# Query products in two column parts, and expert-table products 352 to 400 columns wide, in a two-layer PEER trunk

## The chip, the cores and the metric

The kernel runs on one core of one Trainium2 chip, as one program. The metric is the device time of one execution in microseconds (us), from launch to the last write; smaller is better. One execution was also taken by the hardware profiler, and all rows of a profile below come from that one.

## The reference

The kernel computes two decoder layers for 512 tokens of width 1024. Each layer is a mixer (gated linear attention with memory attention in the first layer, stick-breaking attention with memory attention in the second), a residual with layer norm, and then a PEER feed-forward: every token picks 128 of 16384 experts by product keys and adds up their outputs. The part that matters here, cut down:

```python
def peer(x, w_q, subkeys, u_tab, v_tab):            # x: 512 x 1024
    q = (xf @ w_q).reshape(N, 8, 2, 128)            # 2048 query columns: 16 blocks of 128
    s = einsum('nhpd,hpkd->nhpk', q, subkeys)       # scores against 16 x 128 sub-keys
    top_s, top_i = top_k(s, 16)                     # product keys: 16 x 16 candidates, best 16
    ...
    g = softmax(best_s)
    act = gelu(einsum('nd,nhkd->nhk', xt, u_tab[it]))     # u_tab, v_tab: 16384 x 1024
    return einsum('nhk,nhkd->nd', g * act, v_tab[it])
```

## The kernel before

**How PEER is done.** The kernel treats the tokens in two ways. The first 128 tokens, and 32 of the next 128, gather their experts' rows by indirect DMA and use VectorE. For the other 352 tokens (`TU = 352`, tokens `TU0 = 160` to 511) the product with u's table is done in full on TensorE: all 16384 rows of u, as 128 blocks of 128 rows (`P = 128` blocks), against the 352 tokens. Which experts count, and with what weight, comes in later through gate matrices that are built from one-hot products (`pg`). The v table is then multiplied with the weighted activations for 384 tokens.

**How a product is split.** Each float32 operand is held as a high and a low part of type fp32r (`xhi`, `xlo` for the tokens; `uh`, `ul` for a block of a weight table, made by `split` on ScalarE and VectorE). `stat_mm` computes one block as 24 products: eight 128-row chunks `c` of the contraction, and for each chunk high times high (line 117), high times low (118) and low times high (119). In each of these the block of the weight table is the stationary operand (a weight load of 128 x 128 goes ahead of every product), and the tokens are the moving operand. "Columns" of a product are the columns of the moving operand, that is tokens: 512 for the query products `pq`, 352 for u's products `ph`. `sl` cuts a range out of the columns of both the tokens and the PSUM bank.

**Order of the work.** Per layer there are a stage of query products (16 blocks `pq`, each followed one turn later by four score products `pss` with the sub-keys; the first three blocks, `LEAD = 3`, are done in two halves of 256 columns as the layer norm ahead of them finishes), a stage of u blocks (`ublock(b)`, with the VectorE selection work, the gate products `pg` and the row gathers paced in between by `Stream` budgets), and a stage of v blocks (products `acc`, 512 columns). In the u stage the order on VectorE, ScalarE and TensorE is the order in which the code is written. All 24 products of a block write one PSUM bank of 512 float32 columns (`ps`, 8 banks), which ScalarE reads when the block is done: `query(pn)` for a query block, and a GELU over `ph[:, :TU]` one turn later for a u block.

**Names in the rows.** `pq<-xhi,uh` is a query product, `ph<-xhi,uh` one of u's, `acc` one of v's, `pz` a logit product of the stick-breaking attention (64 rows deep, two at a time on the two halves of the rows), `bsp` and the like are input projections.

Of the kernel before, what the change touches and what calls it, by code (L numbers as in the profile page):

```python
# [18 lines left out]
T = 512  # L19
# [12 lines left out]
def new_x(E):  # L32

    E.xhi = E.xp.tile([P, NC, T], F32R, tag="xhi", name="xhi")
    E.xlo = E.xp.tile([P, NC, T], F32R, tag="xlo", name="xlo")


def setup(ctx, tc):
# [19 lines left out]
    new_x(E)  # L58
    E.raw = ctx.enter_context(tc.tile_pool(name="raw", bufs=RB))
    E.hl = ctx.enter_context(tc.tile_pool(name="hl", bufs=3))  # L60
# [14 lines left out]
def psum(E, name="ps", tag="ps"):  # L75
    p, tags = E.ps
    return p.tile([P, 512], F32, tag=tag, name=name, bufs=tags[tag])
# [31 lines left out]
def stat_mm(E, ps, hi, lo, xhi=None, xlo=None, sl=slice(None), cs=range(NC)):  # L109

    nc = E.nc
    xhi = E.xhi if xhi is None else xhi
    xlo = E.xlo if xlo is None else xlo
    ps = ps[:, sl]
    for c in cs:
        h, l = hi[:, c * P:(c + 1) * P], lo[:, c * P:(c + 1) * P]
        nc.tensor.matmul(ps, h, xhi[:, c, sl], start=(c == 0), stop=False)  # L117
        nc.tensor.matmul(ps, h, xlo[:, c, sl], start=False, stop=False)  # L118
        nc.tensor.matmul(ps, l, xhi[:, c, sl], start=False, stop=(c == NC - 1))  # L119
# [121 lines left out]
def out_proj_ln(E, cat, wo, lng, lnb, ahead, order, w, rows=None):  # L241
# [3 lines left out]
    with E.tc.tile_pool(name="lp", bufs=1, reuse_waits="tile") as lp:  # L245
# [6 lines left out]
        with E.tc.manual_schedule(engines={mybir.EngineType.PE}):  # L252
            accs = [[psum(E, name="oacc") for h in range(2)] for t in range(2)]

            def add(t, cs):
                for c in cs:
                    ch, cl = cat[c]
                    mov_mm(E, accs[t], ch[:, t * P:(t + 1) * P], cl[:, t * P:(t + 1) * P], *w[c], c == order[0], c == order[-1])
# [8 lines left out]
            for t in range(2):  # L267
                add(t, order[2:WOI])
            for t in range(NT + 1):
                if t < 2:  # L270
                    add(t, order[WOI:])
                elif t < NT:
                    accs.append([psum(E, name="oacc") for h in range(2)])
                    add(t, order[:WOI])
                    x_to_T(E, t - 2)
                    add(t, order[WOI:])
                else:
# [717 lines left out]
def x_to_T(E, t, tag="ps"):  # L995

    nc = E.nc
    for g in range(2):
        ps = psum(E, name="xtp", tag=tag)
        for j in range(4):  # L1000
            c = g * 4 + j
            nc.tensor.transpose(ps[:, j * P:(j + 1) * P], E.x[:, t, c * P:(c + 1) * P], E.ident)
        hi = E.xhi[:, g * 4:(g + 1) * 4, t * P:(t + 1) * P]
        lo = E.xlo[:, g * 4:(g + 1) * 4, t * P:(t + 1) * P]
        psv = ps.rearrange("p (j n) -> p j n", j=4)
        nc.scalar.activation(hi, psv, AF.Copy)
        nc.vector.tensor_sub(lo, psv, hi.bitcast(F32))
# [56 lines left out]
TU0 = T0 + SD  # L1064
TU = T - TU0
# [22 lines left out]
LEAD = 3  # L1088
TAIL = 6
G3 = 96  # L1090
WARM = 6
WOI = 3
RB = 4
SEG = [(0, 1, 0, 16), (1, 3, 16, 8), (4, 4, 40, 4), (8, 8, 56, 1)]

# [15 lines left out]
def peer(E, mixer, wq, sk, ut, vt, un, lng, lnb, out_dram=None, follow=()):  # L1111
# [11 lines left out]
    with ExitStack() as pp:  # L1123
        parts = {}

        def prep(i, later=None):

            if i >= 16 + P:
                return
            parts[i] = split(E, load_raw(E, wq[i] if i < 16 else ut[i - 16], "ur"), "u", later=later)  # L1130
# [124 lines left out]
        with ExitStack() as up:  # L1255
# [383 lines left out]
            def select(row):  # L1639

                on = [sel for sel in sels if row < ER or sel is not sels[2]]
                topk16(*[sel.job() for sel in on[:2]])
                if on[2:]:
                    topk16(on[2].job())
                if row % 8 == 7:
                    for sel in on:
                        lead.q.append(candidates(sel))
                        if sel is first and sel.nr == 8:
                            lead.q.append(first.part(0, 4))
                return WF - 1140 - 1175 * len(on)  # L1650

            def query(pq):
                qT = wk.tile([P, T], F32, tag="act", name="qT")
                nc.scalar.activation(qT, pq, AF.Copy)
                return qT

            def scores(r, qT):
                pss = psum(E, name="pss")
                for t in range(NT):
                    nc.tensor.matmul(pss[:, t * P:(t + 1) * P], qT[:, t * P:(t + 1) * P], skt[:, r], start=True, stop=True)  # L1660
                return lambda: nc.scalar.activation(sall[:, r].rearrange("p t k -> p (t k)"), pss, AF.Copy)

            def flush():
                while later:
                    later.pop(0)(V)
# [4 lines left out]
            for r in range(17):  # L1670
                if r < 16:
                    if r < LEAD:
                        pn = pes[r]
                    else:
                        hi, lo = parts.pop(r)
                        pn = psum(E, name="pq")
                        stat_mm(E, pn, hi, lo)
                if r > 0:
                    ev = scores(r - 1, qT)
                if r + 2 >= LEAD:  # L1680
                    prep(r + 2, later if r > 1 else None)
                if r < 16:
                    qT = query(pn)
                if r > 0:
                    ev()
                if r > 1:
                    avail[0] = r - 1
                    lead(select(r - 2))
                    flush()
                    gus(GQ)  # L1690
# [7 lines left out]
            def ublock(b):  # L1698
                nonlocal ab, ph, big, keep, g0
                if b == KB:  # L1700
                    big = gp.tile([P, 16 * NT * P], F32, tag="big", name="keep")
                    keep = big[:, :KEEP * TU].rearrange("p (b n) -> p b n", n=TU)
                    g0 = big[:, KEEP * TU:KEEP * TU + G0 * TD].rearrange("p (s i n) -> p s i n", i=G0, n=TS)
                if 0 < b <= KB:
                    if (b - 1) % AB == 0:
                        ab = wk.tile([P, AB, TU], F32, tag="act", name="act")
                pn = None
                if b < P:
                    if b > 0:
                        prep(b + 18, later)  # L1710
                    hi, lo = parts.pop(16 + b)
                    pn = psum(E, name="ph")
                    stat_mm(E, pn[:, :TU], hi, lo, E.xhi[:, :, TU0:], E.xlo[:, :, TU0:])
                if b > KB:
                    nc.scalar.activation(keep[:, b - 1 - KB], ph[:, :TU], AF.Gelu)
                elif b > 0:
                    nc.scalar.activation(ab[:, (b - 1) % AB], ph[:, :TU], AF.Gelu)
                    if (b - 1) % AB == AB - 1:
                        nc.scalar.dma_start(Ad[(b - 1) // AB], ab)
                ph = pn  # L1720
                gst(GR if work.q else GR2)
                if lead.q:
                    lead(WB0)
                else:
                    work(WB if ready or sready and len(gst.q) > 1 else WB0)
                flush()
                if b < P - 1:
                    gus(GU if work.q else GU2 if b < KB else GU3)
                if LOG:
                    print("block", b, len(work.q), len(gst.q), len(gus.q), gcount)  # L1730

            for b in range(BX):
                ublock(b)
# [72 lines left out]
        with written:  # L1806
            for b in range(BX, P + 1):
                ublock(b)
                if b < P:
                    vprep(b - BX)  # L1810
# [4 lines left out]
            for b in range(P):  # L1815
# [6 lines left out]
                whi, wlo, hi, lo = vp.pop(b)  # L1822
                for t in range(ND):
                    sl = slice(t * P, (t + 1) * P)
# [21 lines left out]
            for t in range(ND):  # L1846
                sl = slice(t * P, (t + 1) * P)
# [43 lines left out]
def trunk(ctx, tc, a, out):  # L1891
    nc = tc.nc
    E = setup(ctx, tc)
    mix = mixer_a(E, a)
    peer(E, mix, a["wq0"], a["sk0"], a["ut0"], a["vt0"], a["un0"], a["lng1"], a["lnb1"], follow=[a["b_st"][b] for b in (0, 1, 12)])
    mix = mixer_b(E, a["b_st"], a["b_nat"], a["b_wo"], a["lng2"], a["lnb2"])
    peer(E, mix, a["wq1"], a["sk1"], a["ut1"], a["vt1"], a["un1"], a["lng3"], a["lnb3"], out_dram=out)
# [58 lines left out]
```

## Time and profile before

| what | value |
|---|---|
| median of 2 runs | 2854.38 us (2854.05 to 2854.7) |
| the profiled execution's own time | 2856.13 us |
| its span, first to last instruction | 2854.1 us |
| granted TensorE clock, mean over the span | 0.997 |
| TensorE products (PE), busy | 2821.5 us, 99% of the span, 16235 instructions |
| TensorE weight loads (PEld), busy | 2501.9 us, 88% |
| VectorE (DVE) / ScalarE (ACT), busy | 2442.0 us, 86% / 1440.4 us, 50% |
| query stage, first layer | from 227.3 us to 331.0 us |
| u stage, first and second layer | 567.0 us and 570.9 us long |

Products overlap in the profile: one of 512 columns in v's stage is shown as 389 ns long, and the next one starts before it ends. So the step from one product's start to the next one's says what a product costs in a stream, and its duration does not. The source rows give the count, the shortest, median and longest duration, and the start of the first and of the last.

### The profile page before, as it was taken

To read this page: it belongs to the slowest core of one execution; us is meant where nothing else is said; L and a number is where in the kernel's file an instruction comes from. 1 tells how busy PE (TensorE), PEld (TensorE's weight loads), DVE (VectorE), ACT (ScalarE), POOL (GpSimd) and SP (SyncE) were. 2 spreads that over 40 slices of the span, in tenths; PEclk is the share of its full clock that TensorE was granted. 3 is DMA by queue.
4 is the path that set the end of the run, shared out by engine and by line. 5 is a ranking of instruction groups with operands and counts; after the bars stand their busy time and mean duration, and the time that the engine had idled before them with its cause. 6 is when DMAs were issued, how large, how long until landed. Compare 5 with 4: busy or idle time off the path is not lost.

```text
span 2854.1 us, 44772 instructions
## 1 busy us (share of the span) xinstructions
PE 2821.5 (99%) x16235; PEld 2501.9 (88%) x16235; DVE 2442.0 (86%) x4866; ACT 1440.4 (50%) x2699; POOL 754.3 (26%) x615
## 2 busy tenths in 40 slices
PE   9999999999999999999999999999999999999998
PEld 8888999999999888888787889999999998888886
DVE  5566999999987888888968779999998878888888
ACT  6342446667674334443346434476776834334332
POOL 0100233333343333333100002333333433234320
PEclk9999999999999999999999999999999999999999
DMA  5332599999999999999621326999999999999994
GB/s 195 111 104 77 190 314 329 337 333 348 352 375 363 346 371 369 388 359 376 223 67 45 111 82 228 330 314 327 332 350 359 368 369 345 373 348 399 364 377 164
DMA packets 317934, 821.26 MB, mean 288 GB/s; under 512 B 34608, under 2 KB 126992, under 8 KB 311312
## 3 DMA queue, kind: packets, MB, share of 16 engines
q1 hardware_dynamic: 198112, 414.24, 41.0%
q0 software_dynamic: 82944, 302.03, 29.4%
q10 hardware_dynamic: 36656, 102.14, 9.3%
q8 instruction: 127, 2.08, 0.3%
q14 instruction: 95, 0.78, 0.1%
HBM read 723.31 MB, written 92.90 MB: 286 GB/s over the span
## 4 chain that ended last, share of the span: by engine, by line
PE 80%; DVE 16%; issue 2%; ACT 1%; DMA 1%; ACTq 0%; POOL 0%; DVEq 0%; SPq 0%; POOLq 0%
PE acc L289 12%; PE acc L291 12%; PE acc L293 12%; PE ph L117 7%; PE ph L119 7%; PE ph L118 7%; DVE gr L1106 4%; DVE ul L1106 4%; DVE ob L1106 2%; PE pq L117 2%; PE pq L118 2%; PE pq L119 2%; PE pss L1660 1%; PE bsp L117 1%; PE oacc L289 1%
## 5 line engine op out<-in xcount | busy, mean ns | idle before, releaser
L119 PE MATMUL ph<-xhi,ul 128*128 128x352 f32 x2048 | 670.5, 327 | 11.3 <-DVE ul L1106 10.9
L117 PE MATMUL ph<-xhi,uh 128*128 128x352 f32 x2048 | 681.5, 333 | 0.0
L118 PE MATMUL ph<-xlo,uh 128*128 128x352 f32 x2048 | 668.3, 326 | 0.0
L1166 POOL DMA_INDIRECT gr<-in_un,gidx x256 | 344.2, 1345 | 1063.5 <-DVE gr L1106 483.6
L97 ACT ACTIVATE vh<-vr 128x1024 fp32r<-128x1024 f32 x248 | 263.1, 1061 | 521.4 <-PE acc L293 481.4
L1166 POOL DMA_INDIRECT gr<-in_vt,gidx x256 | 297.9, 1164 | 613.7 <-DVE va L1245 550.5
L289 PE MATMUL acc<-vh,whi 128*128 128x512 f32 x1480 | 456.0, 389 | 1.4 <-ACT whi L1801 1.4
L293 PE MATMUL acc<-vh,wlo 128*128 128x512 f32 x1480 | 455.8, 389 | 0.0
L291 PE MATMUL acc<-vl,whi 128*128 128x512 f32 x1480 | 455.8, 389 | 0.0
L98 DVE TENSOR_TENSOR vl<-vr,vh 128x1024 fp32r<-128x1024 f32 x248 | 303.5, 1224 | 144.9 <-ACT vh L97 142.3
L97 ACT ACTIVATE uh<-ur 128x1024 fp32r<-128x1024 f32 x288 | 303.9, 1055 | 243.5 <-PE ph L118 198.9
L119 PEld LDWEIGHTS ph<-xhi,ul 128*128 128x128 f32 x2048 | 385.9, 188 | 17.8 <-DVE ul L1106 17.4
L118 PEld LDWEIGHTS ph<-xlo,uh 128*128 128x128 f32 x2048 | 386.6, 189 | 0.0
L117 PEld LDWEIGHTS ph<-xhi,uh 128*128 128x128 f32 x2048 | 386.3, 189 | 0.1
L1106 DVE TENSOR_TENSOR ul<-ur,uh 128x1024 fp32r<-128x1024 f32 x280 | 340.2, 1215 | 10.2 <-ACT uh L97 9.8
L289 PEld LDWEIGHTS acc<-vh,whi 128*128 128x128 f32 x1480 | 277.5, 188 | 60.3 <-ACT whi L1801 3.1
L293 PEld LDWEIGHTS acc<-vh,wlo 128*128 128x128 f32 x1480 | 277.6, 188 | 58.1 <-DVE wlo L1802 0.7
L291 PEld LDWEIGHTS acc<-vl,whi 128*128 128x128 f32 x1480 | 277.6, 188 | 58.0 <-DVE vl L98 0.8
L1106 DVE SCALAR_TENSOR_TENSOR gr<-gr,xnat 128x1024 f32<-128x1024 f32 x256 | 309.4, 1217 | 20.4 <-DMA gr<-in_un,gidx 20.2
L1245 DVE SCALAR_TENSOR_TENSOR va<-gr,gw,va 128x1024 f32<-128x1024 f32 x254 | 324.7, 1278 | 1.1
L1571 ACT ACTIVATE obl<-ob,rat 128x128 f16<-128x128 f16 x704 | 223.9, 392 | 50.5 <-DVE ob L1106 31.6
L1801 ACT ACTIVATE whi<-w 128x384 fp32r<-128x384 f32 x256 | 131.0, 512 | 68.7 <-DVE w L1790 63.2
(388 smaller groups left out, 4325.2 us busy)
## 6 DMA issues: line engine op xcount, KB each, us to landing
ur<-in_ut SPq DMA_DIRECT2D x256, 512.0 KB
vr<-in_vt SPq DMA_DIRECT2D x256, 512.0 KB
Gd<-gt ACTq DMA_DIRECT2D x48, 1024.0 KB
gl<-Gd SPq DMA_DIRECT2D x26, 1536.0 KB
Ad<-act ACTq DMA_DIRECT2D x112, 352.0 KB
al<-Ad SPq DMA_DIRECT2D x112, 352.0 KB
ur<-in_wq SPq DMA_DIRECT2D x32, 512.0 KB
bs<-in_b_st SPq DMA_DIRECT2D x14, 512.0 KB
```

The costliest lines, as they stand in the source:

```text
L97: nc.scalar.activation(hi, raw, AF.Copy)
L98: sub = lambda eng=eng: eng.tensor_sub(lo, raw, hi.bitcast(F32))
L117: nc.tensor.matmul(ps, h, xhi[:, c, sl], start=(c == 0), stop=False)
L118: nc.tensor.matmul(ps, h, xlo[:, c, sl], start=False, stop=False)
L119: nc.tensor.matmul(ps, l, xhi[:, c, sl], start=False, stop=(c == NC - 1))
L289: nc.tensor.matmul(acc[hf], lh, hi[:, hf * 512:(hf + 1) * 512], start=first, stop=False)
L291: nc.tensor.matmul(acc[hf], lh, lo[:, hf * 512:(hf + 1) * 512], start=False, stop=False)
L293: nc.tensor.matmul(acc[hf], ll, hi[:, hf * 512:(hf + 1) * 512], start=False, stop=last)
L1106: self.ins = op(*args, **kw)
L1166: nc.gpsimd.indirect_dma_start(out=gr, out_offset=None, in_=tab, in_offset=bass.IndirectOffsetOnAxis(ap=idx[:, k:k + 1], axis=0))
L1245: nc.vector.scalar_tensor_tensor(va, gr, gw[:, k:k + 1], va, op0=ALU.mult, op1=ALU.add)
L1571: nc.scalar.activation(obl[:, q], ob[:, q, 0], AF.Copy, scale=rat[:, n0 + q:n0 + q + 1])
```

## The change

Two tables of widths are added, and two calls of `stat_mm` change. Of each layer's 16 query blocks the 13 that were done in one go (`r` from 3 to 15) are now done in two column parts: 24 products over the first `QW[r - LEAD]` columns and then 24 over the rest, with every weight chunk loaded twice. The parts are 320 and 192 columns for the first of them, 336 and 176 for the next, and so on; the wide part has 350.8 columns in the mean and the narrow one 161.2. Each u block takes `n = UW[b % 8]` columns, 352, 356, 360, 364, 368, 376, 384 or 400, the last `n` tokens of the 512; the mean is 370. The PSUM view is then cut to its last 352 columns, so the GELU reads the same tokens as before, and the surplus columns are computed and not read.

```diff
+QW = (320, 336, 304, 288, 272, 352, 344, 328, 368, 384, 400, 416, 448)
+UW = (352, 356, 360, 364, 368, 376, 384, 400)
...
                         pn = psum(E, name="pq")
-                        stat_mm(E, pn, hi, lo)
+                        for sl in (slice(0, QW[r - LEAD]), slice(QW[r - LEAD], T)):
+                            stat_mm(E, pn, hi, lo, sl=sl)
...
+                    n = UW[b % len(UW)]
                     pn = psum(E, name="ph")
-                    stat_mm(E, pn[:, :TU], hi, lo, E.xhi[:, :, TU0:], E.xlo[:, :, TU0:])
+                    stat_mm(E, pn[:, :n], hi, lo, E.xhi[:, :, T - n:], E.xlo[:, :, T - n:])
+                    pn = pn[:, n - TU:]
```

On TensorE, the first whole query block (`r = 3`) stands between two groups of score products. Before it reads as follows (24 products, of which the first three are shown):

```order
L1660 MATMUL pss<-skt,qT 128x128 x8
L117 MATMUL pq<-xhi,uh 128x512
L118 MATMUL pq<-xlo,uh 128x512
L119 MATMUL pq<-xhi,ul 128x512
...
L1660 MATMUL pss<-skt,qT 128x128 x4
```

In the changed kernel the same place holds 24 products of 320 columns and 24 of 192:

```order
L1662 MATMUL pss<-skt,qT 128x128 x8
L117 MATMUL pq<-xhi,uh 128x320
L118 MATMUL pq<-xlo,uh 128x320
L119 MATMUL pq<-xhi,ul 128x320
...
L117 MATMUL pq<-xhi,uh 128x192
L118 MATMUL pq<-xlo,uh 128x192
L119 MATMUL pq<-xhi,ul 128x192
...
L1662 MATMUL pss<-skt,qT 128x128 x4
```

Nothing else moved there. TensorE's program has 624 products more in all (2 layers x 13 blocks x 24). The u blocks hold the same number of products as before, 768 of each of the eight widths over both layers. The order of the instructions on VectorE, ScalarE, GpSimd and SyncE is the same as before.

## The prediction

> **What bounds the kernel now.** I read the page's busy line first, then the stages one by one, since the change touches two of them only.
>
> ```profile
> PE 2821.5 (99%) x16235; PEld 2501.9 (88%) x16235; DVE 2442.0 (86%) x4866; ACT 1440.4 (50%) x2699; POOL 754.3 (26%) x615
> 227.30:331.00 103.70, 103.70 (x594) 91.12 (x593) 84.85 (x410) 36.80 (x54) 7.32 (x7) 1.00 0.34 114
> 331.00:898.00 567.00, 560.40 (x3885) 545.91 (x3884) 532.24 (x1217) 366.31 (x743) 208.97 (x152) 1.00 0.95 341
> 1643.80:1747.50 103.70, 103.70 (x594) 91.12 (x593) 84.85 (x410) 36.80 (x54) 6.38 (x7) 1.00 0.38 120
> 1747.50:2318.40 570.90, 563.03 (x3886) 547.55 (x3885) 530.96 (x1214) 364.51 (x742) 205.60 (x152) 0.99 0.94 339
> PE ph L119 <- DVE ul L1106: 10.9, 14, 1.5
> ```
>
> The four windows are the two query stages and the two u stages. Their columns are length, then busy time with the count of PE, PEld, DVE, ACT and POOL. In the query stages PE is busy for all of 103.70 us, so it waits for nobody there. In the u stages it is idle for 567.00 - 560.40 = 6.6 us and 570.90 - 563.03 = 7.9 us, 14.5 us together, of which the last row puts 10.9 us down to VectorE's low parts `ul`. VectorE is nearly full too (532 of 567 us), but it is TensorE that is late nearly all the time. Whatever the change adds to TensorE's stream in these four windows therefore lengthens the run, less what it takes out of those 14.5 us. So the question is what a product costs as a function of its columns, and the answer has to come from steps between starts.
>
> ```profile
> L118 PE MATMUL pq<-xlo,uh x21: 283/283/283, 237.8 to 245.0; 128*128 128x256 f32 x21
> L118 PE MATMUL pq<-xlo,uh x6: 389/389/389, 255.3 to 258.7; 128*128 128x512 f32 x6
> L118 PE MATMUL ph<-xlo,uh x41: 327/328/328, 339.8 to 359.8; 128*128 128x352 f32 x41
> 550.78 0.32 PE L117 MATMUL ph<-xhi,uh 128*128 128x352 f32 x1
> 554.58 0.32 PE L117 MATMUL ph<-xhi,uh 128*128 128x352 f32 x1
> ```
>
> Every third product of a stream is on line 118, so 21 of them are 60 steps: 256 columns cost 7.2 us / 60 = 120.0 ns. The second row gives 3.4 / 15 = 226.7 ns for 512 columns. From these two, a column costs 106.7 / 256 = 0.4167 ns, and each product has 13.3 ns on top. At 352 columns that line would give 160.0 ns, but the trace has **two rhythms** there. The third row, an undisturbed stretch of 120 steps, gives 20.0 / 120 = 166.7 ns. The last two rows stand 24 products apart in a later stretch and give 3.80 / 24 = 158.3 ns. I call these the slow rhythm (20.0 ns above the columns) and the fast one (11.7 ns above). A stream keeps its rhythm until a wait disturbs it.
>
> The mean over a u stage lies between. The first layer's stage of 567.0 us holds 3072 products of u, and these besides:
>
> ```profile
> 331.00:898.00 567.00, 527.39 (x3071) 502.97 (x3072) 56.72 (x127) 1.00 0.95 341
> L1590 PE MATMUL pg<-ob 128*128 128x128 f16 x704 | 95.8, 221 | 0.0
> 702.78 0.23 PE L1590 MATMUL pg<-ob 128*128 128x128 f16 x1
> 703.21 0.41 PE L117 MATMUL ph<-xhi,uh 128*128 128x352 f32 x1
> 703.46 0.33 PE L118 MATMUL ph<-xlo,uh 128*128 128x352 f32 x1
> ```
>
> The first row is for the tile `ph` alone, with its 3072 weight loads. A gate group is 8 products in 703.21 - 702.78 = 0.43 us, and the step after it is 0.25 us, some 0.08 longer than usual. With 704 such products on this line over both layers, as many on the next, and a few of the side tokens, a layer has about 96 groups (an estimate): 41 + 8 = 49 us. With 9 us for waits (the 6.6 of idle time, and some that the overlap covers) and 1 for transposes, 567 - 59 = 508 us remain, that is 165 ns for each product. So about four fifths of the stream is in the slow rhythm.
>
> **The change, part by part.** *Query blocks.* 13 blocks in each of 2 layers, 24 products each, are 624 products of 512 columns, which become 624 wide and 624 narrow ones. The wide parts have 350.8 columns in the mean: 146.2 ns for the columns, and 160 ns with the 13.3 of the two straight rows. With 11.7 they are 158, with 20 they are 166. The narrow parts (64 to 240 columns, 161.2 in the mean) lie below every width that a full-depth stream of this type has in the trace. What bounds them can be seen in the stick-breaking logits, which are products of 512, 384 and 128 columns with the same kind of weight load:
>
> ```profile
> 1502.20 0.34 PE L788 MATMUL pz<-kqh 64*128 64x384 f32 x2
> 1502.38 0.34 PE L788 MATMUL pz<-kql,kqh 64*128 64x384 f32 x2
> 1502.55 0.34 PE L788 MATMUL pz<-kqh,kql 64*128 64x384 f32 x2
> 1502.79 0.27 PE L788 MATMUL pz<-kql,kqh 64*128 64x128 f32 x2
> 1502.90 0.27 PE L788 MATMUL pz<-kqh,kql 64*128 64x128 f32 x2
> 1502.73 0.19 PEld L788 LDWEIGHTS pz<-kql,kqh 64*128 64x128 f32 x2
> 1502.84 0.19 PEld L788 LDWEIGHTS pz<-kqh,kql 64*128 64x128 f32 x2
> ```
>
> At 384 columns the step is 1502.55 - 1502.20 = 0.35 us for two, 175 ns, close to the straight line's 173.3. At 128 columns it is 110 ns where the line has 66.7, and just as far apart stand the two weight loads behind it (1502.73 and 1502.84). So the load is the floor, at about 109 ns. The line reaches that at 230 columns, so 12 of the 13 narrow widths lie on the floor and the 240 costs 113.3; I take 109. A split product then costs 160 + 109 = 269 ns for 226.7 before, 42.3 more, and 624 x 42.3 = **+26.4 us**. The bounds: if the floor of the pairs did not hold for single products, 67.2 + 11.7 = 79 ns with the fast rhythm's 158 would give 624 x 10.2 = +6; a floor of 120 (the shortest full-depth step above) with 166 gives +37. A gain is excluded, since the columns alone take as long as before and a second overhead comes with each.
>
> *u's products.* All 6144 go from 352 to 370 columns in the mean. If every column cost its 0.4167 ns on top of today's 165 it would be 7.5 ns. I do not take that, because the slow rhythm holds 352 columns at a step that the straight line reaches at (166.7 - 13.3) / 0.4167 = 368. So up to 368 columns the surplus can hide in the slack that the slow rhythm leaves. I take 165 for 352, 166 for 356, 360 and 364, 166.7 for 368, and the line's 170.0, 173.3 and 180.0 for 376, 384 and 400. The mean is 1353 / 8 = 169.1, 4.1 more than now, and 6144 x 4.1 = **+25.2 us**. The lower bound is the fast rhythm everywhere, 154.2 + 11.7 = 165.9: +0.9 ns, 5.5 us. The upper bound is the slow rhythm's 20 ns at every width, 174.2: +9.2 ns, 56.5 us. A gain would need less overhead than any row shows. The estimate stands between, nearer to the row of 352 in its slow rhythm, which is the commonest one.
>
> *What is given back.* The stretching leaves VectorE more time for each block (its program is unchanged), so some of the 14.5 us of idle TensorE goes. Waits for a gathered row or a table block do not shrink, so I take half, **-7 us**; the bounds are 0 and -14.5. The v stages and the mixers are untouched. On the other engines a later PSUM bank is all that changes, and ACT, at 366 of 567 us, has room.
>
> The sum is 26.4 + 25.2 - 7 = +44.6 us. The profiled execution took 2856.13 us (2854.1 of span, 2.0 around it), which makes 2900.7. The median of the runs is 1.75 us lower, so I predict **2900 us**, 1.6% slower.
>
> The Trainium skill, "TensorE: Matmul & The Clock Gate", section "Back-to-back issue gap", puts the step of a warm product at its columns over 2.4 GHz and 2.5 ns. The slope of the rows agrees (0.4167 ns a column), the 2.5 does not: it would be 215.8 ns for the 226.7 measured at 512 columns, and 149.2 for 158.3 or 166.7 at 352. By that rule the split alone would cost 624 x 2.5 = 1.6 us and u's surplus the full 46 us, and the run would be 2856 + 48 - 7 = 2897. That is the same total out of other parts, and the parts can be told apart in the new profile.
>
> **The rivals.** (1) *Every surplus column is paid in full.* The two rhythms may belong to each width and not to a fixed step, so that every width lies on average the same 18.3 ns above its columns as 352 does now. Then u costs 7.5 x 6144 = +46, the wide query parts 164.5 and the narrow 109 (46.8 x 624 = +29), and 4 are given back: +71, 2927 us by the profiled run, **2925**. This ends beyond 2% (2911). For it speaks the slow rhythm's share of the stream now; against it that 256 and 512 columns settle at 13.3.
>
> (2) *The fast rhythm.* The odd widths never settle and every product stays near 11.7: u +5.5, query parts 158 + 109 - 226.7 = 40.3, +25, and 8 given back: +22, **2877**. For it speaks that the changing widths disturb a stream at every block; against it the 41 rows of 327 to 328 ns above, a settled stretch.
>
> (3) *Not slower.* The single mechanism is that a narrow product is not held by its weight load, because the loads run ahead during the wide half. Then the query blocks cost only +6, u in the fast rhythm +5.5, and nearly all of the 14.5 us of idle time, say 13, is taken up by it: -1.5, **2853**. It decides from a step of under 80 ns in the narrow parts. Against it stand the two loads 0.11 us apart above, with a product of 384 columns ahead of them.
>
> **How the numbers follow.** Forecast 0.46, (1) 0.25, (2) 0.22, (3) 0.05, and 0.02 for something faster that I cannot name. The forecast's own range is 2887 to 2914. To hold 8 in 10 the range takes in (2) nearly whole and (1) up to the slow rhythm at every width (56.5 + 32 - 4 = +84, 2939) in its lower half: 2871 to 2934. A change of under 2%, 57 us, is about what a measurement of this kernel can tell from none, and the forecast's upper tail crosses it. So slower by over 2% has 0.25 + 0.05 = 0.30, within 2% has 0.69, and faster 0.01.
>
> **What would show it.** In the new profile the narrow rows of `pq` should stand 105 to 112 ns apart whatever their width, and the wide ones on 0.4167 ns a column and 12 to 20 more. The query stages should be 103.7 + 13 = 117 us long and the u stages 567 + 9 and 571 + 9. In the u stages the steps at 356 to 368 columns should be close to those at 352, and at 400 some 13 ns above. PE's idle time in the u stages should fall below 14.5 us. The forecast is wrong if a width of 356 to 400 settles more than 20 ns above its columns, for instance because an odd start of the moving operand (byte 624 or 592 of a row) costs extra, or if the narrow parts come out at their columns' 27 to 100 ns.

## The result, and the profile after

The changed kernel takes **2896.97 us** (2896.82 to 2897.11) against 2854.38 us before: a ratio of 1.0149, 95% interval 1.0106 to 1.0193, so 42.6 us or 1.5% slower. The forecast was 2900 us within 2871 to 2934.

The stages first: the two query stages and the two u stages of the changed kernel, with the columns as in the windows of before, and below them TensorE's waits for the low parts of u's blocks.

```profile
227.45:344.66 117.21, 117.21 (x907) 116.74 (x906) 85.24 (x410) 36.66 (x54) 7.72 (x7) 1.00 0.33 108
344.66:920.61 575.95, 573.41 (x3886) 559.10 (x3885) 531.33 (x1214) 364.40 (x742) 204.57 (x150) 1.00 0.93 335
1666.28:1783.49 117.21, 117.21 (x907) 116.73 (x906) 85.17 (x410) 36.67 (x54) 6.57 (x7) 1.00 0.35 113
1783.49:2359.56 576.07, 573.57 (x3887) 559.33 (x3886) 533.67 (x1218) 365.75 (x743) 205.87 (x151) 1.00 0.93 335
PE ph L119 <- DVE ul L1108: 3.7, 7, 0.8
```

Each query stage went from 103.70 to 117.21 us, 27.0 us for both. The u stages went from 567.00 and 570.90 to 575.95 and 576.07, 14.1 us together. The rest of the program is where it was: the span grew by 41.0 us, from 2854.1 to 2895.1. PE's idle time in the u stages fell from 14.5 us to 2.54 + 2.50 = 5.0, and the waits for `ul` from 10.9 to 3.7 us. VectorE is as busy as before, 531 to 534 us a stage.

In the query stages the narrow parts stand on the floor that the logits had shown. Here are three products of 64 columns and the weight loads around them, then three of 448 columns:

```profile
341.16 0.28 PE L117 MATMUL pq<-xhi,uh 128*128 128x64 f32 x1
341.27 0.28 PE L118 MATMUL pq<-xlo,uh 128*128 128x64 f32 x1
341.38 0.28 PE L119 MATMUL pq<-xhi,ul 128*128 128x64 f32 x1
341.25 0.19 PEld L118 LDWEIGHTS pq<-xlo,uh 128*128 128x128 f32 x1
341.36 0.19 PEld L119 LDWEIGHTS pq<-xhi,ul 128*128 128x128 f32 x1
341.47 0.19 PEld L117 LDWEIGHTS pq<-xhi,uh 128*128 128x128 f32 x1
339.00 0.37 PE L117 MATMUL pq<-xhi,uh 128*128 128x448 f32 x1
339.21 0.37 PE L118 MATMUL pq<-xlo,uh 128*128 128x448 f32 x1
339.42 0.37 PE L119 MATMUL pq<-xhi,ul 128*128 128x448 f32 x1
```

Products and loads alike are 0.11 us apart, where 64 columns alone would take 27 ns. All thirteen narrow widths, 64 to 240 columns, have steps of 108 to 112 ns in the mean of their blocks, so up to 240 columns the width makes no difference. That the load is what sets this floor is read from the equal spacing; no run here changes the stationary operand of these products. The three products of 448 columns are 0.21 us apart; in the mean of such a block, its first step left out, it is 206.4 ns, 6 above the straight line, while the other wide widths lie within about 2 of it. The Trainium skill ("TensorE: Matmul & The Clock Gate", section "LDWEIGHTS (loading the stationary operand)") puts a load at its columns over 1.2 GHz, an estimate of 106.7 ns here; the 0.11 us of the rows is close above it.

In the u stage each block has its own width, so the starts of successive blocks, 24 products apart, give the step of each width directly:

```profile
344.66 0.41 PE L117 MATMUL ph<-xhi,uh 128*128 128x352 f32 x1
348.55 0.32 PE L117 MATMUL ph<-xhi,uh 128*128 128x356 f32 x1
352.39 0.33 PE L117 MATMUL ph<-xhi,uh 128*128 128x360 f32 x1
356.39 0.33 PE L117 MATMUL ph<-xhi,uh 128*128 128x364 f32 x1
360.32 0.33 PE L117 MATMUL ph<-xhi,uh 128*128 128x368 f32 x1
364.32 0.33 PE L117 MATMUL ph<-xhi,uh 128*128 128x376 f32 x1
368.47 0.34 PE L117 MATMUL ph<-xhi,uh 128*128 128x384 f32 x1
372.63 0.34 PE L117 MATMUL ph<-xhi,uh 128*128 128x400 f32 x1
377.03 0.32 PE L117 MATMUL ph<-xhi,uh 128*128 128x352 f32 x1
```

360 columns cost 4.00 us / 24 = 166.7 ns and 368 the same, 384 cost 4.16 / 24 = 173.3, and 400 cost 4.40 / 24 = 183.3, which is 3.3 more than the straight line. Over both stages, with waits and the first step after a gate group left out, the means are 159.9 (352), 165.1, 166.3, 165.2, 166.9, 173.1, 173.8 and 183.3 ns (400), 169.2 in all. The same count in the run before gives 164.2.

### The profile page after: what moved, and what is told of

Read it like the earlier page. It is cut to its first block, busy times and chain, and to the rows that moved or that the text cites. A ratio compares the mean times of both kernels' runs of the same rounds, so it can differ in the third digit from the quotient of the medians.

```text
span 2895.1 us, 46022 instructions
## 1 busy us (share of the span) xinstructions
PE 2872.0 (99%) x16859; PEld 2578.0 (89%) x16859; DVE 2444.8 (84%) x4866; ACT 1438.3 (50%) x2699; POOL 742.8 (26%) x615
## 4 chain that ended last, share of the span: by engine, by line
PE 79%; DVE 17%; issue 2%; DMA 1%; ACT 1%; POOL 0%; ACTq 0%; DVEq 0%; SPq 0%; POOLq 0%
PE acc L289 11%; PE acc L291 11%; PE acc L293 11%; PE ph L117 7%; PE ph L119 7%; PE ph L118 7%; DVE gr L1108 4%; DVE ul L1108 4%; PE pq L118 2%; PE pq L119 2%; PE pq L117 2%; DVE ob L1108 2%; PE pss L1662 1%; PE bsp L117 1%; PE oacc L289 1%
## 5 line engine op out<-in xcount | busy, mean ns | idle before, releaser
L117 PE MATMUL ph<-xhi,uh 128*128 128x352 f32 (+7 forms) x2048 | 690.8, 337 | 0.0
L119 PE MATMUL ph<-xhi,ul 128*128 128x352 f32 (+7 forms) x2048 | 678.9, 331 | 3.8 <-DVE ul L1108 3.7
L118 PE MATMUL ph<-xlo,uh 128*128 128x352 f32 (+7 forms) x2048 | 677.4, 331 | 0.0
L1168 POOL DMA_INDIRECT gr<-in_vt,gidx x256 | 288.6, 1127 | 623.3 <-DVE va L1247 560.2
L117 PE MATMUL pq<-xhi,uh 128*128 128x256 f32 (+26 forms) x512 | 152.8, 298 | 0.0
```

Source lines behind the costliest of these rows:

```text
L1168: nc.gpsimd.indirect_dma_start(out=gr, out_offset=None, in_=tab, in_offset=bass.IndirectOffsetOnAxis(ap=idx[:, k:k + 1], axis=0))
```

## The experiments

Steps below are means over all of u's products but the first after another kind of product, with steps beyond 200 ns counted as waits. "Waits" are what those steps have over a normal one, in both u stages; they come out larger than PE's idle time because the product ahead of a wait covers some of it. In the run before they are 22.4 us (8.8 and 13.6), in the changed kernel 6.9.

**One half at a time.** The first kernel keeps the query part of the diff alone, the second u's part alone; both edits are shown against the changed kernel.

```diff
 # first kernel
-                    n = UW[b % len(UW)]
-                    stat_mm(E, pn[:, :n], hi, lo, E.xhi[:, :, T - n:], E.xlo[:, :, T - n:])
-                    pn = pn[:, n - TU:]
+                    stat_mm(E, pn[:, :TU], hi, lo, E.xhi[:, :, TU0:], E.xlo[:, :, TU0:])
 # second kernel
-                        for sl in (slice(0, QW[r - LEAD]), slice(QW[r - LEAD], T)):
-                            stat_mm(E, pn, hi, lo, sl=sl)
+                        stat_mm(E, pn, hi, lo)
```

> The query half of the change alone: 13 query blocks a layer in two parts of the thirteen widths, u's products at 352 columns as before. Plain sum: the two query stages go from 103.7 to 117.2 us each and nothing else moves, +27 us, 2881 us. Rival (a longer query stage gives VectorE a head start into the u stage): some of the 22 us that u's products wait in the run before goes away here already, 2866 to 2875 us, with u stages of 560 to 565 us instead of 567 and 571.

> The other half alone: u's products 352 to 400 columns wide in turn, query products undivided. Plain sum: u's steps go from 164.2 to 169.2 ns in the mean (+31 us) and TensorE's waits in the u stages shrink by some 15 us, because each block leaves VectorE more time: +14 to +16 us, 2869 us, u stages of 576 us. Rival (the waits shrank because the query stages were longer): the waits stay near 22 us here, +29 us, 2883 us, u stages of 583 to 586 us.

The query half took 2881.14 us, a ratio of 1.009 (1.0073 to 1.0107), and u's half 2870.2 us, 1.0051 (1.0031 to 1.0071). First a query stage and a u stage of the first kernel, then the u stages of the second:

```profile
227.12:344.33 117.21, 117.21 (x907) 116.74 (x906) 85.24 (x410) 36.68 (x54) 7.72 (x7) 1.00 0.33 109
344.33:913.53 569.20, 560.74 (x3886) 544.92 (x3885) 531.94 (x1217) 365.17 (x743) 206.96 (x151) 1.00 0.94 339
330.95:906.72 575.77, 573.66 (x3887) 559.39 (x3885) 533.37 (x1218) 365.64 (x743) 205.03 (x152) 1.00 0.94 337
1756.89:2332.92 576.03, 573.50 (x3887) 559.29 (x3886) 531.96 (x1216) 365.15 (x742) 204.36 (x152) 1.00 0.94 335
```

The halves add up: 26 and 15 us against 42.6 for both. The longer query stage takes no wait away, since PE is still idle for 8.5 us of the first kernel's u stage (6.6 before). u's wider products alone take them away (2.1 and 2.5 us of idle time). So the plain sums hold and both rivals fall.

**A split without narrow parts.** Query blocks in two halves of 256 columns, both above the load's floor.

```diff
-                        stat_mm(E, pn, hi, lo)
+                        for sl in (slice(0, T // 2), slice(T // 2, T)):
+                            stat_mm(E, pn, hi, lo, sl=sl)
```

> As before the change, with the 13 query blocks split into two parts of 256 columns, both above the weight load's floor. If a split costs one more 13.3 ns of overhead and the rest of the query change was the floor of the narrow parts, a query stage is 24 x 13 x 13.3 ns = 4.2 us longer than 103.7, 107.9 us, where the thirteen widths made it 117.2; the whole +8 us, 2863 us. If loading every weight chunk twice costs time by itself, the stage is near 117 us here too.

```profile
227.13:334.47 107.34, 107.34 (x907) 107.29 (x906) 84.96 (x410) 36.66 (x54) 7.74 (x7) 1.00 0.34 114
```

The stage is 107.34 us, 3.6 longer than 103.70 (2861.41 us in one run). It has as many products and loads as the changed kernel's stage of 117.21, so about a quarter of the query term is the second overhead, and three quarters are the floor under the narrow parts.

**All of u's products at 400 columns.** The query blocks are whole again here, as before the change; the edit is shown against the changed kernel.

```diff
-UW = (352, 356, 360, 364, 368, 376, 384, 400)
+UW = (400,)
...
-                        for sl in (slice(0, QW[r - LEAD]), slice(QW[r - LEAD], T)):
-                            stat_mm(E, pn, hi, lo, sl=sl)
+                        stat_mm(E, pn, hi, lo)
```

> Every one of u's products 400 columns wide (the last 400 tokens, 48 surplus columns not read), query products undivided. If a width has a step of its own that a stream settles on, as the changed kernel's rows have it (183.3 ns at 400 for u): +19.1 ns x 6144 = 117 us, less 17 us of waits, 2954 us. If the step of 183.3 came from the blocks of other widths around it, it settles at the 180.0 that the query part of 400 columns has: +97 - 17, 2934 us.

It took 2947.04 us, 1.0324 (1.0307 to 1.0342). A stretch of the u stage and the whole stage:

```profile
L118 PE MATMUL ph<-xlo,uh x37: 345/345/345, 340.0 to 359.8; 128*128 128x400 f32 x37
330.94:945.43 614.49, 614.39 (x3887) 599.86 (x3886) 536.00 (x1219) 366.86 (x743) 197.05 (x152) 1.00 0.90 316
```

108 steps in 19.8 us are 183.3 ns again, without any neighbour of another width, so the 3.3 ns above the line are not handed on from other blocks. The steps cost +18.9 x 6144 = 116 us; 21 of the 22 us of waits are gone (0.1 us of idle time is left in each stage); the total is a little below the expected 2954.

**The start in the row.** In the change a wider product also starts further to the front (`T - n`), and the query part of 352 columns, which starts at column 0, ran at 160.0 ns throughout. So I moved the start with the width kept, and then the widths with the start kept.

```diff
 # 352 columns from column 128
-                    stat_mm(E, pn[:, :TU], hi, lo, E.xhi[:, :, TU0:], E.xlo[:, :, TU0:])
+                    stat_mm(E, pn[:, :TU], hi, lo, E.xhi[:, :, 128:128 + TU], E.xlo[:, :, 128:128 + TU])
 # eight starts in turn
+US = (160, 128, 0, 64, 32, 96, 144, 152)
...
+                    n0 = US[b % len(US)]
+                    stat_mm(E, pn[:, :TU], hi, lo, E.xhi[:, :, n0:n0 + TU], E.xlo[:, :, n0:n0 + TU])
 # the eight widths from column 0
...
+                    n = UW[b % len(UW)]
...
+                    stat_mm(E, pn[:, :n], hi, lo, E.xhi[:, :, :n], E.xlo[:, :, :n])
```

> As before the change, but u's products take columns 128 to 479 of the tokens instead of 160 to 511: 352 columns that start at another place of the row (the activations are then those of other tokens). If the slow rhythm belongs to 352 columns, nothing changes: steps of 158.3 and 166.7 ns, 164.2 in the mean, 2854 us. If it belongs to the start in the row, the steps are the 160.0 of the query part of 352 columns, which starts at column 0: 4.2 ns x 6144 = 26 us less, 2828 us, perhaps a few more where VectorE then is late.

> Before the change, but block by block u's 352 columns start at column 160, 128, 0, 64, 32, 96, 144 and 152 of the tokens in turn (only the first of these gives the right activations; the place in the row is all that differs). If only starts that are whole multiples of 128 columns (512 bytes) are good, the blocks at 128 and 0 settle at 160.0 ns and all others at 158 or 166.7 or between. If a multiple of 64 or 32 columns is enough, 64 (and 32, 96 and 160) join them. If a stream's rhythm is handed on from block to block and the start has no part in it, all eight starts have the same mixture.

> The changed kernel's eight widths for u, all starting at column 0 instead of ending at column 511 (so other tokens' activations), query products undivided. If the start makes the staircase, 352, 368, 384 and 400 columns lie on the straight line here, 160.0, 166.7, 173.3 and 180.0 ns, and 356, 360 and 364 between 160 and 166.7; the mean is about 167.5 ns instead of 169.2. If the widths make it, the steps are those of the changed kernel: 167 at 356, 360 and 368, 173 at 376 and 384, 183 at 400.

From column 128 the run took 2846.61 us, 0.9973 (0.9961 to 0.9984). A stretch of its u stage, and both u stages:

```profile
L118 PE MATMUL ph<-xlo,uh x42: 322/323/324, 340.0 to 359.7; 128*128 128x352 f32 x42
330.67:892.68 562.01, 550.19 (x3887) 533.42 (x3885) 531.48 (x1216) 364.15 (x742) 208.14 (x152) 1.00 0.95 343
1742.02:2305.61 563.59, 550.89 (x3887) 533.55 (x3885) 530.60 (x1214) 363.10 (x740) 207.85 (x152) 1.00 0.95 342
PE ph L119 <- DVE ul L1106: 21.3, 19, 1.7
```

123 steps in 19.7 us are 160.2 ns, and the mean of the run is 160.4: the two rhythms are gone. Yet only 8 us are gained of 3.8 x 6144 = 23, and the expected 2828 us are missed by 19. PE now idles 11.8 + 12.7 = 24.5 us, 10 more than before, and waits twice as long for `ul`. (The profiled execution, at 2843.48 us, was the fastest of seven; its two u stages are 12.3 us shorter than before, about 23 less 10.)

With eight starts in turn (2854.84 us in one run) the block starts show it within one stretch. From here on four blocks start at column 160, 128, 0 and 64, and the last two rows are another block at 160 and its end:

```profile
362.12 0.32 PE L117 MATMUL ph<-xhi,uh 128*128 128x352 f32 x1
366.11 0.32 PE L117 MATMUL ph<-xhi,uh 128*128 128x352 f32 x1
369.97 0.33 PE L117 MATMUL ph<-xhi,uh 128*128 128x352 f32 x1
373.84 0.33 PE L117 MATMUL ph<-xhi,uh 128*128 128x352 f32 x1
...
396.10 0.32 PE L117 MATMUL ph<-xhi,uh 128*128 128x352 f32 x1
399.90 0.32 PE L117 MATMUL ph<-xhi,uh 128*128 128x352 f32 x1
```

The block at 160 takes 3.99 us once and 3.80 us the other time (166 and 158 ns), the ones at 128 and 0 take 3.86 and 3.87 (161). Over all 256 blocks, in the settled part of each (its last two thirds), the starts 0, 64, 128 and 144 give 160 to 161 ns every time. 160, 32 and 96 are mostly 158 or 167 from block to block, and 152 gives 162 to 163. So the rhythm belongs to the start, and the three starts that are whole multiples of 64 columns (256 bytes) are free of the slow one. 144, a multiple of 16 alone, is free of it too, which that rule does not explain.

With the eight widths from column 0 (2866.32 us in one run), the starts of three successive blocks, of 384, 400 and 352 columns, read:

```profile
355.18 0.34 PE L117 MATMUL ph<-xhi,uh 128*128 128x384 f32 x1
359.34 0.34 PE L117 MATMUL ph<-xhi,uh 128*128 128x400 f32 x1
363.66 0.32 PE L117 MATMUL ph<-xhi,uh 128*128 128x352 f32 x1
```

400 columns take 4.32 us / 24 = 180.0 ns here for 183.3 at start 112, and 384, which start at column 128 in the changed kernel, take the same 173.3 in both. But the mean only fell to 168.3, not to 167.5: 364 columns cost 166.7 and 376 cost 173.1 from column 0 too.

| columns | from T - n, as changed (start) | from column 0 | straight line |
|---|---|---|---|
| 352 | 159.9 (160) | 160.8 | 160.0 |
| 356 | 165.1 (156) | 160.5 | 161.7 |
| 360 | 166.3 (152) | 164.1 | 163.3 |
| 364 | 165.2 (148) | 166.7 | 165.0 |
| 368 | 166.9 (144) | 167.1 | 166.7 |
| 376 | 173.1 (136) | 173.1 | 170.0 |
| 384 | 173.8 (128) | 173.7 | 173.3 |
| 400 | 183.3 (112) | 180.3 | 180.0 |

The rows that fell are 356 by 4.6, 360 by 2.2 and 400 by 3.0 ns; 364 rose by 1.5. So the start is one cause. The width seems to be another, since 376 columns lie 3 ns above the line from both starts, but only two starts of each width were tried.

**A version with the better start.** To start 352 columns at column 128 and keep the right tokens, PEER's token columns 128 to 511 were stored 32 columns further to the front, with the 32 gathered tokens at the end of the row.

```diff
+ROT = 32
...
+    elif t == 1:
+        cuts = [(0, ROT, T - ROT), (ROT, P, P)]
+    else:
+        cuts = [(0, P, t * P - ROT)]
...
-                nc.scalar.activation(qT, pq, AF.Copy)
+                nc.scalar.activation(qT[:, :P], pq[:, :P], AF.Copy)
+                nc.scalar.activation(qT[:, P:P + ROT], pq[:, T - ROT:], AF.Copy)
+                nc.scalar.activation(qT[:, P + ROT:], pq[:, P:T - ROT], AF.Copy)
...
+                    stat_mm(E, pn[:, :TU], hi, lo, E.xhi[:, :, P:P + TU], E.xlo[:, :, P:P + TU])
```

> A version that computes all of the reference: inside PEER the token columns 128 to 511 are stored 32 columns further to the front (the 32 gathered tokens of the second tile go to the end of the row), so that the 352 columns start at column 128; the query result is put back in order by three copies instead of one, and the two early parts are 224 and 288 columns wide. If the start is the cause, u's steps are 160.4 ns and the time is that of the run with start 128, plus some 2 us for the extra copies: 2843 to 2850 us, a ratio of 0.996 to 0.998 to the kernel before. If the gain came from the wrong tokens' data and not from the start, 2855 us or more.

> The version that computes all of the reference, with one step put in order: in the first layer two parts of the concatenated heads lie in the columns that the second tile's tokens are written to, so there that tile is written only after the last tile's products have read them. As with the stored columns turned before: u's steps 160.4 ns at start 128 for 164.2, some 23 us less of PE's stream, of which 10 to 12 come back as waits for VectorE: 2845 to 2850 us, ratio 0.996 to 0.998. If the start were not the cause, 2855 us or more.

The first of the two took 2848.04 us, 0.9977 (0.9967 to 0.9986). In it, in the first layer, the second tile's columns were written over two parts of the heads that the last tile's products had yet to read, so it leaves out part of that tile's sum. In the second, that tile is written later. It took 2851.6 us, **0.9993 (0.9984 to 1.0002)**, no measurable gain. Its u stages:

```profile
333.14:900.15 567.01, 551.35 (x3886) 533.52 (x3884) 530.42 (x1214) 363.40 (x740) 208.05 (x152) 1.00 0.95 341
1752.27:2314.95 562.68, 550.28 (x3887) 533.26 (x3885) 530.46 (x1214) 363.43 (x740) 207.86 (x152) 1.00 0.95 343
PE ph L119 <- DVE ul L1119: 22.0, 20, 1.7
```

The steps are 160.4 ns as expected, but 15.7 + 12.4 = 28.1 us of idle time stand against 14.5 before. The expectation, 0.996 to 0.998, was missed by 3 to 4 us. The two u stages are 8.2 us shorter together, but the first of them begins 2.1 us later than before, and the stretch between the two is 2.6 us longer; the turned layout's extra copies and the later write lie there.

**Is it VectorE that takes the gain back?** To test this, VectorE's product with each gathered row of u was halved, which leaves out half of each dot product, once with each start.

```diff
-                V.scalar_tensor_tensor(gr, gr, 1.0, xr, op0=ALU.mult, op1=ALU.mult, accum_out=dst[:, k:k + 1])
+                V.scalar_tensor_tensor(gr[:, :D // 2], gr[:, :D // 2], 1.0, xr[:, :D // 2], op0=ALU.mult, op1=ALU.mult, accum_out=dst[:, k:k + 1])
```

> As before the change, but VectorE's product of a gathered row of u with the tokens covers 512 of its 1024 columns (half of each dot product is left out), which takes some 0.55 us of 1.2 us from 160 instructions a layer; gathers and all other work stay. If the waits of TensorE in the u stages come from VectorE's load, nearly all of the 22 us go: 2832 to 2838 us. If they come from the transfers that VectorE itself waits for, they stay: 2848 to 2855 us. It also gives the price of u's stages without waits, for the next kernel.

> The same half product, and u's 352 columns start at column 128 (other tokens' activations). If VectorE's load is what took back most of the gain of the better start, the whole 3.8 ns x 6144 = 23 us show here: 23 us less than the run with the half product at start 160, some 2810 to 2815 us, and fewer than 5 us of waits. If the stretch between the two starts is only some 8 us again, VectorE's load is not what takes it back.

They took 2838.92 us, 0.995 (0.9934 to 0.9967), and 2813.49 us, 0.986 (0.9844 to 0.9877). Here are the busy times of the first of them and its wait for `ul`:

```profile
PE 2816.4 (99%) x16235; PEld 2502.8 (88%) x16235; DVE 2279.2 (80%) x4866; ACT 1438.4 (51%) x2699; POOL 702.7 (25%) x615
PE ph L119 <- DVE ul L1106: 1.0, 4, 0.3
```

VectorE is busy for 2279.2 us instead of 2442.0, and the waits in the u stages fell from 22.4 to 2.6 us although every gather stayed. So they came from VectorE's load and not from the transfers. The difference between the two starts is 25.4 us, where it had been 8 us with VectorE's full load. By the steps of before (164.2 ns against 160.4) it would be 23 us, and by those of the first of these two, which rose to 165.1 ns, 29. Of the second only the time is known, so what is left of its waits stays open.

The rise to 165.1 ns goes with the fewer waits. Followed product by product, the run before has 14 places where a slow stretch ran into a wait, and at 11 of them it went on in the fast rhythm. Of the 21 changes from the fast rhythm to the slow one, 20 came across a group of gate products without a wait. That rise is why the first lies just above the expected 2832 to 2838.

## Why the prediction was right

- *What bounds the kernel* held. Both halves of the change land on TensorE's stream, and its cost was the number of steps times their length, less the waits that went.
- *Query blocks*: predicted +26.4 us, measured +27.0. The wide parts were put at 160 ns and the narrow at 109, and the run shows 108 to 112 for the narrow and the straight line within about 2 ns for the wide, 6 at 448 columns. The floor, taken from the row of 128-column logits, held down to 64 columns.
- *u's products*: predicted +25.2 us less 7, measured +14.1. The new mean was 169.1 in the text and is 169.2 in the run, but this hides errors that cancel: 352 fell to 159.9 instead of staying at 165, 400 came to 183.3 instead of 180.0, and 376 to 173.1 instead of 170.0. The old mean was set a little too high: 165 from the stage's length less its other parts, and 164.2 when counted step by step. So the steps cost 5.0 x 6144 = 30.7 us, 5.5 more than the term. That the mean came out right is luck.
- *What is given back* is the term that was mis-sized: -7 us, bounded at -14.5, measured -15.5 (22.4 to 6.9 us). PE's idle time was taken for the whole of the waits, though the product ahead covers part of each. And half of them were thought to be transfers, while the run with the halved product shows that nearly all of them (22.4 to 2.6 us) were VectorE's load. The term's error of 8.5 us and the 5.5 us of the steps cancel in part, so the total of 42.6 us came nearer to the forecast's 44.6 than its parts did.
- *The reason given for u's estimate*, that the slow rhythm's slack hides up to 368 columns, gave the right mean without being the cause: in the changed kernel 352 columns cost 159.9 ns in the mean, and the wider ones up to 368 cost 5 to 7 ns more. 352 columns run at 160.4 ns when they start at column 128. The start in the row and the width both set the step. The prediction named an odd start only as something that could spoil it. Of a stream it said that the rhythm holds until a wait disturbs it, but in the run before the groups of gate products change it too.
- *Of the signs it named*, the query stages (117 us), the narrow steps and the smaller idle time came true. Two did not: the steps at 356 to 368 columns are not close to those at 352, and 400 columns lie 23 ns above 352 and not 13.
- *The rivals*: 18.3 ns above the columns at every width (1) and 11.7 everywhere (2) are both refuted by the table. Loads that run ahead of narrow parts (3) are refuted by the loads 0.11 us apart.
- The 2.5 ns on top of the columns that the Trainium skill states ("TensorE: Matmul & The Clock Gate", section "Back-to-back issue gap"; it calls this the gap of an isolated product), weighed in the prediction, is not what any of u's widths here shows; the table has 12 to 17 ns.
- *The sum* gives 2899 us as it stands (2900.7 less 1.75), where 2900 was written. And a change of under 2% can be told from none here: the interval begins at 1.0106, and even the 0.27% of the run that starts at column 128 is clear of 1.

## What to carry to other kernels

Price a stream of products by the steps between their starts, per width and per start of the moving operand, and take a narrow part (64 to 240 columns, with a new 128 x 128 weight load each) at no less than the 108 to 112 ns measured here. Before counting a gain on the busiest engine, ask how close the next one is: here 23 us less of TensorE's stream brought 8, because VectorE is busy for 531 of 562 us. The same closeness makes a loss cheaper, 31 us of longer steps costing 14.

## What the runs showed of the hardware that was not expected

Where the moving operand starts in its row changes the step of otherwise equal products: 352 columns from a start of 0, 64, 128 or 144 columns settle at 160 to 161 ns, and from 32, 96 or 160 they mostly fall into 158 or 167 ns. From column 160, waits mostly led out of the slow rhythm (11 of 14) and groups of gate products back into it (20 of 21). 400 columns cost 180.0 ns from column 0 and 183.3 from column 112. What in the chip does this was not tested.
